# Placing work around a recurrent chain by a queue model that keeps an engine's occupation and a result's latency apart, with later low parts, SA copied by ScalarE and scores as a part of their own

## The chip, the cores and the metric

The kernel runs on one core of a Trainium2 chip. The metric is the device time of one execution in microseconds. The engines are called as the profile calls them: PE is TensorE (PEld its weight loads), DVE is VectorE, ACT is ScalarE, POOL is GpSimd, and SP is SyncE, which here only issues DMAs.

## The reference

One layer of a hybrid decoder runs on 2048 new tokens of a prompt and on 8 sequences of 4 tokens that have a state. The width is 1024, with 16 heads of 64.

```python
h = _rmsnorm(x, norm_g)
p = jnp.einsum('bsd,dn->bsn', h, w_in)
p_conv, p_rwkv, p_gate = _split(p, [N_CONV_COLS, N_RWKV_COLS, 2 * D_MODEL])
...
def step(S, inp):
    r_t, k_t, v_t, d_t, kk_t, a_t = inp
    sa = jnp.einsum('bhvk,bhk->bhv', S, -kk_t)
    S = (S * d_t[:, :, None, :] + sa[..., None] * (kk_t * a_t)[:, :, None, :]
         + v_t[..., None] * k_t[:, :, None, :])
    y = jnp.einsum('bhvk,bhk->bhv', S, r_t)
    return S, y
...
pc = jnp.einsum('bsc,cd->bsd', y_c, w_out_c)
pr = jnp.einsum('bsc,cd->bsd', y_r, w_out_r)
m = jax.nn.sigmoid(gc) * pc + jax.nn.sigmoid(gr) * pr
out = jnp.einsum('bsd,de->bse', m, w_o)
return x + out, ...
```

Beside the recurrent branch there is a short convolution branch (`y_c`). All is float32.

## The kernel before, in words

**Main stream.** The projections `p` are matmuls of weight blocks of 128 columns with the normalised input. To keep float32 accuracy with fast matmuls, each weight block and the input are split in a high and a low part, and three products are summed: `proj` issues, for each of eight k steps, high x high, low x high and high x low, 24 matmuls into one PSUM tile `ip`. The high part of a weight is a copy by ScalarE (`A.copy(hl[:, 0], raw)`), the low part a subtraction on VectorE (`w_lows`, tile `whl`). Both are stored, so that only the first of the four token sets (512 tokens each, the last with the 32 sample tokens added, called sets 0 to 3) splits weights; the others load the parts. `w_lows` is called at k step 2 of each block, and before a block's first use.

**Side jobs.** For each set and each of eight head pairs p there is a job per stage: *keys* (decay, scan, and the scaled keys AR, BK), *solve* (the scores `pt<-AR,BK`, their masking to GM, the 32 x 32 blocks Mc, their transpose Mi, and 31 pairs of operations tt, X that invert a triangular block), *merge* (the inverse Xbd), *load* (SV and BKt transposed) and *chain*. The chain carries the state S of a pair through 8 chunks of 64 tokens, one step each, and each link needs the one before: pa = AR x S on PE, us on DVE (two operations, one per head), pb = Xbd x us on PE, two copies into SV (`inner`: one by DVE, one by ACT), pb = BKt x SV on PE, S on DVE (two operations), and again pa. The matmuls of the main stream are put between the links, to cover them.

**Who decides the order.** The order of the instructions on each engine is that in which the Python code emits them, and a planner within the code decides it. `Traced` records each operation and its cost in `Clock`, which holds a time for each engine and for each part of a tile when it is ready. `drive` goes through the main stream matmul by matmul and, after each, lets each live `Side` run some steps: it runs when its goal (its share of the pair's stretch, from CUTS and SIDES) asks for it, when its next step's inputs are ready by the clock no later than PE's time (`due`), and, if it isn't one of the urgent kinds, when DVE is less than BACKLOG (1800) ahead of PE. `need` runs a job to its end when a tile must be free. Costs are by number of elements: for DVE 150 + 1.05 per element, for ACT 200 + 0.84. In `Clock.add` an engine is busy until the result is there, and what another engine reads is ready 60 later (200 behind PE). The framework's own scheduler moves rows of DVE and ACT a little afterwards.

All recorded operations have the line of the one call in `Traced`, L117 in the profile, so that the tiles tell them apart. `Queue` issues the DMAs on SP (L168).

After the last chain there is phase 3: the output projections `pc`, `pr` and `out`, again in split parts, with their 24 weights (tiles RH, RL, gt, ML, po) split on the way.

Of the kernel before, what the change touches and what calls it, by code (L numbers as in the profile page):

```python
# [23 lines left out]
HN = NT // 2  # L24
SIDES = {"first": 8.0, "late": 14.0, "keys": 30.0, "solve": 30.0, "merge": 8.0, "load": 8.0, "samp": 20.0, "out": 12.0, "prep": 10.0, "y": 4.0, "chain": 45.0, "zero": 1.0}

# [11 lines left out]
class Clock:  # L38
# [47 lines left out]

    def add(self, eng, outs, ins, cost, lag=60.0):
        start = max([self.t[eng]] + [e[4] for ap in ins for e in self._hits(ap) if e[6] != eng] +
                    [e[5] for ap in outs for e in self._hits(ap)])
        if eng == "POOL" or eng == "DVE" and sum(ap.space != PSUM for ap in ins) > 1:  # L90
            for s, e in self.held["POOL" if eng == "DVE" else "DVE"]:
                if s < start + cost and start < e:
                    start = e
            self.held[eng] = self.held[eng][-60:] + [(start, start + cost)]
        end = start + cost
        self.t[eng] = end
        for ap in ins:
            for e in self._hits(ap):
                e[5] = max(e[5], end)
        for ap in outs:  # L100
            for p0, p1, f0, f1 in self.boxes(ap):
                old = self.log.setdefault(self.name(ap), [])
                old[:] = [e for e in old if not (p0 <= e[0] and e[1] <= p1 and f0 <= e[2] and e[3] <= f1)][-95:]
                old.append([p0, p1, f0, f1, end + lag, end, eng])


class Traced:
# [18 lines left out]
    def cost(self, op, out, ins, k):  # L126
# [13 lines left out]
        if self.name == "DVE":  # L140
            per = {"transpose": 1.6, "tensor_tensor_scan": 2.1}.get(op, 1.05)
            if op == "tensor_reduce":
                n = ins[0].free_size()
            return 150 + per * n
        if self.name == "ACT":
            return 200 + 0.84 * n + 90 * max(0, len(ins) - 1)
        if k.get("op") == ALU.pow:
# [28 lines left out]
def hybrid_kernel(tc, x_prompt, x_sample, state_conv, state_shift, state_rwkv, norm_g, w_in, conv_w,  # L176
# [10 lines left out]
    NB = D // P  # L187
# [56 lines left out]

    def w_lows():
        while lows:
            hl, raw, keep = lows.pop(0)
            V.tensor_tensor(out=hl[:, 1], in0=raw, in1=hl[:, 0].bitcast(F32), op=ALU.subtract)
            SP.store(keep, hl.bitcast(F32))
# [12 lines left out]
    def proj(w, mov, c0, n):  # L262
# [3 lines left out]
        for kt in range(NB):  # L266
            if kt == 2:
                w_lows()
            for i, (w_, m_) in enumerate(((wh, mh), (wl, mh), (wh, ml))):
                T.matmul(ps[:, :n], lhsT=w_[:, kt, :], rhs=m_[:, kt], start=kt + i == 0, stop=kt == NB - 1 and i == 2)  # L270
                yield n / NT / 3
# [33 lines left out]
    class Side:  # L305
# [14 lines left out]

        def run(self, upto, force=False):
# [3 lines left out]
            while self.given < goal and self.f0 <= upto and (force or max(self.due, pt_free(self.banks)) <= clock.t["PE"] and (  # L325
                    self.kind in URGENT or clock.t["DVE"] < clock.t["PE"] + BACKLOG)):
                try:
                    x = next(self.g)
# [442 lines left out]
    def rkvz_blocks(th, p):  # L771
# [8 lines left out]
        def al(nm, bufs, kind, back):  # L780
            def alloc():
                need(job.get((kind, th * NB + p - back)))
                return rw.tile([P, NT + NSAMP], F32, name=nm, bufs=bufs)
# [20 lines left out]
    def rwkv_keys(th, p, o):  # L804
# [88 lines left out]
        for cvw, pw, ln, dst in parts:  # L893
# [11 lines left out]
        V.scalar_tensor_tensor(out=kh[:, 0:nt], in0=rT[:, 0:nt], scalar=rkh[:, p:p + 1], in1=kh[:, 0:nt],  # L905
                               op0=ALU.mult, op1=ALU.mult)
        yield W["key"], [kh[:, 0:nt]]
        bh = tmp.tile([P, TW], F32R, name="tmp")
# [16 lines left out]

    def rwkv_solve(th, p, o):

# [6 lines left out]
        for c0 in range(0, NCH + samp, 4):  # L934
# [12 lines left out]
            yield W["score"], (), 2 if c0 + 4 < NCH + samp else 0  # L947


# [23 lines left out]
        V.transpose(Xo.rearrange("p a e c -> p (a e c)"), X.rearrange("p a b -> p (a b)"))  # L973
        o.update(GM=GM, Xo=Xo, Mo=Mo)
        yield W["inv"]
# [385 lines left out]
    def begin_pair(th, p, total):  # L1361
# [174 lines left out]
```

## Time and profile before

| | |
|---|---|
| Median of 3 runs | 3245.81 us (3242.76 to 3250.17) |
| Profiled execution, its own time | 3239.32 us |
| Its span | 3237.6 us |
| Mean granted clock of PE | 0.987 |
| Instructions in the span | 54951 |
| Chain that ended last, by engine | PE 67%, DVE 20%, ACT 5%, issue 5%, DMA 2%, POOL 1% |
| DMA | 606.66 MB, mean 187 GB/s |

The page lists busy time per engine. In a row of the timeline stand the start, the duration, engine, line, operation, output tile <- input tiles, shape and how many are merged into the row, and in brackets how long the engine had been idle and who ended that. Rows of the waits name the waiting operation, what it waited for, the total in us, how often, and the longest. In the rows of the groups, after the bar, stand the busy time in us, the mean in ns, and the idle time of the engine ahead of the group, with what ended most of it. By the timeline, the first set runs to about 700 us, sets 1 and 2 from there to about 1900, set 3 to about 2608, the end of the last chain to about 2683, and phase 3 to the end.

### The profile page before, as it was taken

The page shows a single profiled execution, that of the slowest core. Times are in us where ns is not written, and L with a number is a line of the kernel's source. Part 1 is how long each engine was busy: PE and PEld are TensorE (multiplying, and loading weights), DVE is VectorE, ACT ScalarE, POOL GpSimd, SP SyncE. Part 2 cuts the span into 40 slices and gives each one's busy share as a digit, 9 for nine tenths or more (in the row PEclk, how much of TensorE's full clock was granted, in tenths as well). Part 3 has the DMA queues.
Part 4 walks back from the last instruction along what each step waited for, and adds up shares of the span by engine and source line. Part 5 has one row for each costly group of instructions (what it writes and reads, how often), then busy time and mean ns, then how long its engine had stood idle before and what let it go on. Part 6 is the DMA issues. An engine that isn't in the chain of part 4 may idle for free.

```text
span 3237.6 us, 54951 instructions
## 1 busy us (share of the span) xinstructions
PE 3109.5 (96%) x21234; PEld 2585.9 (80%) x21234; DVE 1999.7 (62%) x5703; ACT 1243.0 (38%) x2580; POOL 308.7 (10%) x517
## 2 busy tenths in 40 slices
PE   7999999999999999999999999999999969999998
PEld 6777777877777778777777899888898847788897
DVE  5687777776666657666666676666777745433332
ACT  5454544444334443443433344443444422211201
POOL 2011111110000111110001010100100000000000
PEclk9999999999999999999999999999999979999999
DMA  7786667644444444444444444434433339988773
GB/s 265 256 269 210 223 221 222 213 158 143 152 161 157 157 155 173 155 159 149 158 157 157 145 159 140 133 135 136 139 130 132 122 126 320 351 307 312 265 257 119
DMA packets 233308, 606.66 MB, mean 187 GB/s; under 512 B 32906, under 2 KB 136451, under 8 KB 179286
## 3 DMA queue, kind: packets, MB, share of 16 engines
q1 hardware_dynamic: 232902, 602.61, 54.4%
q8 instruction: 168, 2.75, 0.3%
q14 instruction: 94, 0.77, 0.1%
q0 software_dynamic: 144, 0.52, 0.0%
HBM read 447.90 MB, written 155.17 MB: 186 GB/s over the span
## 4 chain that ended last, share of the span: by engine, by line
PE 67%; DVE 20%; ACT 5%; issue 5%; DMA 2%; POOL 1%; SPq 0%; ACTq 0%; DVEq 0%; POOLq 0%
PE ip L117 48%; PE pt L117 10%; PE po L117 6%; DVE X L117 3%; DVE tt L117 3%; PE pb L117 3%; DVE tmp L117 2%; ACT tmp L117 2%; DVE Mi L117 2%; DVE whl L117 1%; DVE us L117 1%; DVE S L117 1%; PE pa L117 1%; ACT Xbd L117 1%; DVE GM L117 1%
## 5 line engine op out<-in xcount | busy, mean ns | idle before, releaser
L117 PE MATMUL ip<-XH,whl 128*128 128x512 f32 (+3 forms) x7408 | 2053.4, 356 | 6.6 <-DVE whl L117 1.9
L117 PEld LDWEIGHTS ip<-XH,whl 128*128 128x128 f32 x7408 | 1287.3, 190 | 183.2 <-issue 28.4
L117 PE MATMUL ip<-XL,whl 128*128 128x512 f32 (+3 forms) x3704 | 1316.1, 355 | 2.6 <-POOL XL L117 2.6
L117 PEld LDWEIGHTS ip<-XL,whl 128*128 128x128 f32 x3704 | 702.6, 190 | 80.4 <-issue 6.2
L117 DVE TENSOR_TENSOR X<-X,tt 128x60 f32<-128x60 f32 (+24 forms) x992 | 211.4, 213 | 27.4
L117 DVE TENSOR_TENSOR tt<-Mi,X 128x60 f32<-128x60 f32 (+24 forms) x992 | 209.8, 212 | 28.0
L117 DVE SCALAR_TENSOR_TENSOR S<-pb,pe,sp 64x64 f32<-64x64 f32 x512 | 143.6, 281 | 101.7 <-PE pb L117 95.5
L117 ACT ACTIVATE sp<-S,pe 128x128 f32<-128x128 f32 x256 | 99.5, 399 | 258.2 <-DVE S L117 254.9
L117 ACT ACTIVATE tmp<-ip,vec 128x512 f32<-128x512 f32 (+2 forms) x174 | 103.1, 593 | 231.4 <-PE ip L117 230.0
L117 ACT COPY SV<-pb 64x64 f32<-64x64 f32 x256 | 53.3, 208 | 330.2 <-DVE SV L117 326.3
L117 PE MATMUL ip<-RH,whl 128*128 128x512 f32 (+2 forms) x640 | 170.3, 355 | 4.9 <-ACT RH L117 4.9
L117 PE MATMUL po<-whl,MH 128*128 128x512 f32 x544 | 170.7, 394 | 1.2 <-ACT whl L117 1.1
L117 DVE TENSOR_TENSOR whl<-wraw,whl 128x1024 fp32r<-128x1024 f32 x105 | 134.2, 1279 | 53.3 <-ACT whl L117 52.8
L117 DVE SCALAR_TENSOR_TENSOR gt<-gt,ip 128x512 f32<-128x512 f32 (+1 forms) x80 | 46.9, 586 | 169.3 <-PE ip L117 167.1
L117 DVE TENSOR_TENSOR us<-pa,P 64x64 f32<-64x64 f32 x512 | 110.1, 215 | 57.5 <-PE pa L117 38.4
L117 ACT CAST whl<-wraw 128x1024 fp32r<-128x1024 f32 x105 | 109.5, 1044 | 60.6 <-DMA wraw<-in_w_out_r_dram 25.5
L117 PEld LDWEIGHTS pb<-us,Xbd 128*128 128x128 f32 x512 | 86.4, 190 | 57.6 <-PE ip L117 19.7
L117 PEld LDWEIGHTS ip<-RH,whl 128*128 128x128 f32 x640 | 112.8, 189 | 23.7 <-issue 4.0
L117 PEld LDWEIGHTS pb<-SV,BKt 128*128 128x128 f32 x512 | 85.3, 190 | 57.4 <-ACT SV L117 48.7
L117 PE MATMUL pb<-SV,BKt 128*128 128x128 f32 x512 | 108.1, 293 | 18.6 <-ACT SV L117 18.2
L117 PEld LDWEIGHTS po<-whl,MH 128*128 128x128 f32 x544 | 102.1, 188 | 25.6 <-ACT whl L117 1.6
L117 DVE TENSOR_TENSOR GM<-pt,mask_p 128x512 f32<-128x512 f32 x128 | 82.4, 685 | 61.4 <-PE pt L117 61.4
(489 smaller groups left out, 3940.5 us busy)
## 6 DMA issues: line engine op xcount, KB each, us to landing
wraw<-in_w_in_dram SPq DMA_DIRECT2D x81, 512.0 KB
whl<-w_k SPq DMA_DIRECT2D x24, 1024.0 KB
whl<-w_r SPq DMA_DIRECT2D x24, 1024.0 KB
whl<-w_v SPq DMA_DIRECT2D x24, 1024.0 KB
whl<-w_z SPq DMA_DIRECT2D x24, 1024.0 KB
whl<-w_xin SPq DMA_DIRECT2D x24, 1024.0 KB
whl<-w_cg SPq DMA_DIRECT2D x24, 1024.0 KB
whl<-w_zc SPq DMA_DIRECT2D x24, 1024.0 KB
```

The costliest lines, as they stand in the source:

```text
L117: r = f(*a, **k)
```

## The change

Five edits, all in the planner or in where an operation is put; the same matmuls are issued.

1. A cost may be a pair: the time for which the engine is taken, and the time until the result is there. DVE is taken for 80 less than its cost, ACT for 100 less. What an engine reads of its own results is waited for (to the end plus 30; not PE). The costs of DVE's transpose and of ACT are set anew.
2. `w_lows(late)`: from k step 2 a low part is queued when its cast is ready by the clock, and at the latest at k step 5. Before, it was queued at k step 2 whatever the cast.
3. In `inner`, ACT makes both SV copies.
4. The scores are a job of their own (`rwkv_scores`, "score"), with a stretch of its own ahead of the solve; the next pair's keys wait for the score instead of the solve.
5. `need_rows` runs a pair's keys, when its rT or kT tile must be free, only to the step that has read them.

```diff
     def add(self, eng, outs, ins, cost, lag=60.0):
+        taken, cost = cost if isinstance(cost, tuple) else (cost, cost)
         start = max([self.t[eng]] + [e[4] for ap in ins for e in self._hits(ap) if e[6] != eng] +
+                    [e[7] + 30 for ap in ins for e in self._hits(ap) if e[6] == eng != "PE"] +
                     [e[5] for ap in outs for e in self._hits(ap)])
...
         end = start + cost
-        self.t[eng] = end
+        self.t[eng] = start + taken
...
-                e[5] = max(e[5], end)
+                e[5] = max(e[5], start + taken)
...
-                old.append([p0, p1, f0, f1, end + lag, end, eng])
+                old.append([p0, p1, f0, f1, end + lag, start + taken, eng, end])
...
         if self.name == "DVE":
-            per = {"transpose": 1.6, "tensor_tensor_scan": 2.1}.get(op, 1.05)
...
-            return 150 + per * n
+            t = 150 + {"transpose": 1.85 if n > 512 else 1.15, "tensor_tensor_scan": 2.1}.get(op, 1.05) * n
+            return t - 80, t
         if self.name == "ACT":
-            return 200 + 0.84 * n + 90 * max(0, len(ins) - 1)
+            t = 150 + 0.85 * n + 95 * max(0, len(ins) - 1) + 40 * (ins[0].space != PSUM)
+            return t - 100, t
...
-    def w_lows():
-        while lows:
+    def w_lows(late=True):
+        while lows and (late or clock.ready([lows[0][0][:, 0]]) <= clock.t["DVE"]):
...
         for kt in range(NB):
-            if kt == 2:
-                w_lows()
+            if kt >= 2:
+                w_lows(kt >= NB - 3)
...
+    def need_rows(k):
+        sd = job.get(("keys", k))
+        if sd and not sd.ended:
+            need(*sd.after)
+            sd.run(float("inf"), True, lambda: outs[k].get("read"))
...
-        V.tensor_copy(SV[0:64, c, 0:64], pb[0:64, 0:64])
+        A.copy(SV[0:64, c, 0:64], pb[0:64, 0:64])
         A.copy(SV[0:64, c, 64:128], pb[64:128, 0:64])
...
-        job["keys", k] = Side(rwkv_keys(th, p, o), "keys", [prior("load", k - 1), prior("solve", k - 1)] + read(k - 2)).over(0, f[3])
-        job["solve", k] = Side(rwkv_solve(th, p, o), "solve", [job["keys", k], prior("merge", k - 1)] + read(k - 2)).over(f[3], f[4])
+        job["keys", k] = Side(rwkv_keys(th, p, o), "keys", [prior("load", k - 1), prior("score", k - 1)] + read(k - 2)).over(0, f[3])
+        mid = f[3] + 0.1 * total
+        job["score", k] = Side(rwkv_scores(th, p, o), "score", [job["keys", k]] + read(k - 2)).over(f[3], mid)
+        job["solve", k] = Side(rwkv_solve(th, p, o), "solve", [job["score", k], prior("merge", k - 1)]).over(mid, f[4])
```

What it does to the order is seen at three places on DVE. The first is in a steady pair of set 2, at the start of a chain; `tmp<-rst,tmp` is the scan of the keys job, S_471 the state of the chain, `ss` the keys' norms. Before:

```order
L117 TENSOR_TENSOR us<-pa,P_14314 64x64 x2
L117 TENSOR_SCALAR ss<-pt 128x8
L117 RECIPROCAL ss<-ss 128x8
L117 COPY SV<-pb 64x64
L117 SCALAR_TENSOR_TENSOR S_471<-pb,pe,sp 64x64 x2
L117 SCALAR_TENSOR_TENSOR tmp<-rst,tmp 128x512
L117 TENSOR_TENSOR us<-pa,P_14314 64x64 x2
```

The same place after the change:

```order
L120 TENSOR_TENSOR us<-pa,P_14314 64x64 x2
L120 TENSOR_SCALAR ss<-pt 128x8
L120 RECIPROCAL ss<-ss 128x8
L120 SCALAR_TENSOR_TENSOR tmp<-rst,tmp 128x512
L120 SCALAR_TENSOR_TENSOR S_471<-pb,pe,sp 64x64 x2
L120 TENSOR_TENSOR us<-pa,P_14314 64x64 x2
```

SV has left DVE, and the scan stands ahead of S. On PE, the lora matmuls whose result the scan needs stand two main matmuls earlier, ahead of pb.

The second place is in the same pair, where the solve begins (Mi, then the pairs tt, X). Before:

```order
L117 STREAM_TRANSPOSE Mi<-Mc 128x1024
L117 COPY SV<-pb 64x64
L117 TENSOR_TENSOR tt<-Mi,X 128x31
L117 TENSOR_TENSOR X<-X,tt 128x31
L117 TENSOR_TENSOR tt<-Mi,X 128x30
L117 TENSOR_TENSOR X<-X,tt 128x30
L117 TENSOR_TENSOR tt<-Mi,X 128x29
L117 TENSOR_TENSOR X<-X,tt 128x29
L117 TENSOR_TENSOR tt<-Mi,X 128x28
L117 SCALAR_TENSOR_TENSOR S_471<-pb,pe,sp 64x64 x2
```

And after the change:

```order
L120 STREAM_TRANSPOSE Mi<-Mc 128x1024
L120 TENSOR_TENSOR tt<-Mi,X 128x31
L120 TENSOR_TENSOR X<-X,tt 128x31
L120 TENSOR_TENSOR tt<-Mi,X 128x30
L120 TENSOR_TENSOR X<-X,tt 128x30
L120 TENSOR_TENSOR tt<-Mi,X 128x29
L120 TENSOR_TENSOR X<-X,tt 128x29
L120 TENSOR_TENSOR tt<-Mi,X 128x28
L120 TENSOR_TENSOR X<-X,tt 128x28
L120 SCALAR_TENSOR_TENSOR S_471<-pb,pe,sp 64x64 x2
```

Eight operations instead of seven stand between Mi and S. Between S and the next us there are seven instead of six.

The third place is the same point in a pair of set 0. Before:

```order
L117 SCALAR_TENSOR_TENSOR S_474<-pb,pe,sp 64x64 x2
L117 STREAM_TRANSPOSE Mi<-Mc 128x1024
L117 TENSOR_TENSOR us<-pa,P_4029 64x64 x2
L117 TENSOR_TENSOR tt<-Mi,X 128x31
L117 TENSOR_TENSOR X<-X,tt 128x31
L117 COPY SV<-pb 64x64
```

After the change (`whl<-wraw,whl` is a low part):

```order
L120 TENSOR_TENSOR us<-pa,P_3949 64x64 x2
L120 STREAM_TRANSPOSE Mi<-Mc 128x1024
L120 TENSOR_TENSOR tt<-Mi,X 128x31
L120 TENSOR_TENSOR X<-X,tt 128x31
L120 TENSOR_TENSOR whl<-wraw,whl 128x1024
L120 SCALAR_TENSOR_TENSOR S_474<-pb,pe,sp 64x64 x2
```

Mi stood ahead of us and now stands behind it, with a low part between it and S.

On PE, between two steps of the chain in a steady pair there were mostly six main matmuls from pa to pb, six to eight from pb to pb, and seven to the next pa; there now are six, six and seven. In the tail (the last pair's chain, with the last 48 main matmuls), four steps had no main matmul beside them and now three have none.

More of the change, by code (lines that the diff above doesn't have):

```diff
@@ L24 @@
 HN = NT // 2
-SIDES = {"first": 8.0, "late": 14.0, "keys": 30.0, "solve": 30.0, "merge": 8.0, "load": 8.0, "samp": 20.0, "out": 12.0, "prep": 10.0, "y": 4.0, "chain": 45.0, "zero": 1.0}
+SIDES = {"first": 8.0, "late": 14.0, "keys": 30.0, "score": 8.0, "solve": 22.0, "merge": 8.0, "load": 8.0, "samp": 20.0, "out": 12.0, "prep": 10.0, "y": 4.0, "chain": 45.0, "zero": 1.0}
 W = {"sq": 1.0, "norm": 1.0, "lora": 2.0, "one": 1.0, "scan": 2.0, "exp": 2.0, "key": 1.0, "bones": 1.5,
@@ L91, in add @@
             for s, e in self.held["POOL" if eng == "DVE" else "DVE"]:
-                if s < start + cost and start < e:
+                if s < start + taken and start < e:
                     start = e
-            self.held[eng] = self.held[eng][-60:] + [(start, start + cost)]
+            self.held[eng] = self.held[eng][-60:] + [(start, start + taken)]
         end = start + cost
-        self.t[eng] = end
+        self.t[eng] = start + taken
         for ap in ins:
             for e in self._hits(ap):
-                e[5] = max(e[5], end)
+                e[5] = max(e[5], start + taken)
         for ap in outs:
@@ L319, in over, with run @@
             return self
-        def run(self, upto, force=False):
+        def run(self, upto, force=False, passed=None):
             if any(not x.ended for x in self.after) or upto < self.f0:
@@ L326, in run @@
                     self.kind in URGENT or clock.t["DVE"] < clock.t["PE"] + BACKLOG)):
+                if passed and passed():
+                    break
                 try:
@@ L781, in alloc @@
             def alloc():
-                need(job.get((kind, th * NB + p - back)))
+                if kind == "keys":
+                    need_rows(th * NB + p - back)
+                else:
+                    need(job.get((kind, th * NB + p - back)))
                 return rw.tile([P, NT + NSAMP], F32, name=nm, bufs=bufs)
@@ L906, in rwkv_keys @@
                                op0=ALU.mult, op1=ALU.mult)
+        o["read"] = True
         yield W["key"], [kh[:, 0:nt]]
@@ L924, in hybrid_kernel, with rwkv_scores @@
     blk = [(slice(64 * h + 32 * b, 64 * h + 32 * b + 32)) for h in range(2) for b in range(2)]
-    def rwkv_solve(th, p, o):
+    def rwkv_scores(th, p, o):
         AR = o["AR"]
@@ L947, in rwkv_solve @@
             yield W["score"], (), 2 if c0 + 4 < NCH + samp else 0
+        o["GM"] = GM
+    def rwkv_solve(th, p, o):
+        GM = o["GM"]
         Mc = rw.tile([P, NCH, 32], F32, name="Mc")
@@ L973, in rwkv_solve @@
         V.transpose(Xo.rearrange("p a e c -> p (a e c)"), X.rearrange("p a b -> p (a b)"))
-        o.update(GM=GM, Xo=Xo, Mo=Mo)
+        o.update(Xo=Xo, Mo=Mo)
         yield W["inv"]
```

## The prediction

> **What bounds the kernel now.** I read the page's busy times first, then the busy time by stretches, then TensorE's (PE's) waits, and last the timeline at two chain steps.
>
> ```profile
> PE 3109.5 (96%) x21234; PEld 2585.9 (80%) x21234; DVE 1999.7 (62%) x5703; ACT 1243.0 (38%) x2580; POOL 308.7 (10%) x517
> ```
>
> PE is busy 96% of the span, with the same matmuls before and after the change, so only its idle time can go. The stretches (busy us of PE, PEld, DVE, ACT, POOL, then granted clock, DMA share, GB/s) show where it lies: sets 1 and 2, the end of the last chain, and phase 3.
>
> ```profile
> 700.00:1900.00 1200.00, 1176.74 (x7891) 938.03 (x7892) 779.09 (x2355) 484.97 (x1021) 130.13 (x231) 1.00 0.45 156
> 2608.00:2683.00 75.00, 46.50 (x225) 30.03 (x224) 38.14 (x87) 22.27 (x51) 5.58 (x4) 0.68 0.39 128
> 2683.00:3237.00 554.00, 538.76 (x2667) 452.41 (x2667) 204.06 (x383) 96.67 (x177) 11.43 (x17) 0.99 0.77 277
> ```
>
> The waits of PE over the whole run (total, times, longest) name what the change can reach: the three links of the chain.
>
> ```profile
> PE pb L117 <- DVE us L117: 23.8, 41, 1.6
> PE pb L117 <- ACT SV L117: 18.2, 29, 1.4
> PE pa L117 <- DVE S L117: 4.8, 8, 0.9
> ```
>
> They sum to 46.8 us, 1.4% of the run, and that is the whole prize of a better order. Per pair they are small. The first two lines below are all of the chain's waits in a steady pair (1379.00 to 1453.80), the next two those in a pair of set 0 (462 to 540), where weights are still split.
>
> ```profile
> PE pb L117 <- ACT SV L117: 0.7, 1, 0.7
> PE pb L117 <- DVE us L117: 0.3, 1, 0.3
> ...
> PE pb L117 <- DVE us L117: 1.7, 2, 1.1
> PE pb L117 <- ACT SV L117: 0.4, 1, 0.4
> ```
>
> The rows understate a stall a little, since the modelled end of the matmul ahead of it reaches into it: about 0.16 us each (below, pb1 due at 1418.74 + 1.62 = 1420.36 starts at 1420.78, 0.42 late, and its row says 0.26).
>
> **Part by part.** *SA copied by ScalarE.* VectorE (DVE) loses 256 copies, ScalarE gains 256:
>
> ```profile
> L117 DVE COPY SV<-pb 64x64 f32<-64x64 f32 x256 | 53.3, 208 | 38.2 <-PE pb L117 36.2
> L117 ACT COPY SV<-pb 64x64 f32<-64x64 f32 x256 | 53.3, 208 | 330.2 <-DVE SV L117 326.3
> ```
>
> ScalarE's copy already waited for VectorE's (326.3 us of idle time, by the second row), so the two ran one after the other, 0.42 us in all; two on ScalarE take the same 0.42. What goes is the case in which VectorE comes late to its copy: 0.7 idle per steady pair, about 0.85 with the hidden part. It is 53 us off an engine that is not the bound, and 53 us onto one that is busy 38%.
>
> *The order around the chain, steady pairs.* Rows at two places of one steady pair; pa, us, pb, SV, pb, S, pa is one step:
>
> ```profile
> 1386.48 0.38 PE L117 MATMUL pb<-SV,BKt 128*128 128x128 f32 x2
> 1386.90 0.58 DVE L117 SCALAR_TENSOR_TENSOR S<-pb,pe,sp 64x64 f32<-64x64 f32 x2 [2.70 <-PE pb L117]
> 1387.03 0.63 ACT L117 ACTIVATE tmp<-tmp 128x512 f32<-128x512 f32 x1
> 1387.76 1.22 DVE L117 TENSOR_TENSOR_SCAN tmp<-rst,tmp 128x512 f32<-128x512 f32 x1 [0.28 <-ACT tmp L117]
> 1388.34 0.38 PE L117 MATMUL pa<-S,AR 128*128 128x128 f32 x2
> ...
> 1413.41 0.38 PE L117 MATMUL pa<-S,AR 128*128 128x128 f32 x2
> 1413.83 0.45 DVE L117 TENSOR_TENSOR us<-pa,P 64x64 f32<-64x64 f32 x2
> 1414.31 2.07 DVE L117 STREAM_TRANSPOSE Mi<-Mc 128x1024 f32<-128x1024 f32 x1
> 1415.03 0.33 PE L117 MATMUL pb<-us,Xbd 128*128 128x64 f32 x2
> 1416.42 0.19 DVE L117 TENSOR_TENSOR tt<-Mi,X 128x31 f32<-128x31 f32 x1
> ...
> 1416.78 0.49 PE L117 MATMUL pb<-SV,BKt 128*128 128x128 f32 x2
> 1417.77 0.19 DVE L117 TENSOR_TENSOR tt<-Mi,X 128x28 f32<-128x28 f32 x1
> 1417.87 0.57 DVE L117 SCALAR_TENSOR_TENSOR S<-pb,pe,sp 64x64 f32<-64x64 f32 x2
> 1418.74 0.38 PE L117 MATMUL pa<-S,AR 128*128 128x128 f32 x2
> ...
> 1419.94 0.21 DVE L117 TENSOR_TENSOR X<-X,tt 128x50 f32<-128x50 f32 x1
> 1420.19 0.45 DVE L117 TENSOR_TENSOR us<-pa,P 64x64 f32<-64x64 f32 x2
> 1420.78 0.41 PE L117 MATMUL pb<-us,Xbd 128*128 128x64 f32 x2 [0.26 <-DVE us L117]
> ```
>
> From them: pa starts 0.42 before us (1413.41, 1413.83); pa to pb1, with six main matmuls (ip) between, 1.62; pb2 to S 0.42 and, with seven matmuls, to the next pa 1.86 (1386.48, 1388.34), so an ip is 1.86 / 8 = 0.233. A solve operation takes 0.225 (six steps from 1416.42 to 1417.77), the wider ones about 0.24. us ends 0.14 before pb1 can start.
>
> Scan first: the order now puts the scan ahead of S, and the lora matmuls two ip (0.47) earlier. So the scan is ready near 1387.76 - 0.47 = 1387.29 and ends at 1388.51. S then ends 0.58 later, less 0.08 of overlap, at 1389.01, and pa comes at 1389.06 instead of 1388.34: +0.72.
>
> Solve: with SV gone, eight solve operations instead of seven stand between Mi and S, so S starts at 16.42 + 8 x 0.225 = 18.22 and ends at 18.80; pb2 is free to go at 15.03 + 1.62 = 16.65, its pa is due at 18.51, and comes at 18.85, 0.33 late. Seven operations instead of six stand ahead of the next us, which ends at 18.80 + 1.69 + 0.48 = 20.97 while pb1 is due at 18.85 + 1.62 = 20.47: with the 0.14, 0.64 late. The third step has 0.13 left. Sum 1.1.
>
> After: 1.1 + 0.72 = 1.8 a pair. Before: 0.85 for SV, 0.43 for us, 0.1 at 1418.74, 1.4. So +0.4 a pair, and +6 us over the 14 pairs of sets 1 and 2 that repeat this order.
>
> *Set 0.* Mi stood ahead of us there, and pb waited:
>
> ```profile
> 414.87 2.05 DVE L117 STREAM_TRANSPOSE Mi<-Mc 128x1024 f32<-128x1024 f32 x1 [0.61 <-ACT Mc L117]
> 416.95 0.45 DVE L117 TENSOR_TENSOR us<-pa,P 64x64 f32<-64x64 f32 x2
> 417.54 0.41 PE L117 MATMUL pb<-us,Xbd 128*128 128x64 f32 x2 [1.12 <-DVE us L117]
> ```
>
> That is about 1.3 with the hidden part. Now us goes first, and Mi, two solve operations and often a low part stand between us and S: 2.05 + 0.45 + 1.2 = 3.7 from us's end at pa + 0.87, so S is done at pa + 5.2 against pa due at 1.62 + 1.62 + 1.86 = 5.1. That costs 0.1 to 0.15; other places of the new order, where a low part lands ahead of S, give back about as much again. I take -1.0 a pair, for 7 pairs -7 us (bounds -1.3 and +0.4, the steady loss).
>
> *Low parts.* Each low part takes 1.28 us, and VectorE sat idle ahead of it for the cast, 52.8 us in 105:
>
> ```profile
> L117 DVE TENSOR_TENSOR whl<-wraw,whl 128x1024 fp32r<-128x1024 f32 x105 | 134.2, 1279 | 53.3 <-ACT whl L117 52.8 <-DMA xo<-in_x_prompt_dram 0.2
> PE ip L117 <- DVE whl L117: 1.9, 2, 1.1
> ```
>
> Queued when the cast is due, it blocks nothing behind it; that is part of set 0's gain above. Forced at the sixth of eight k steps, it has nine matmuls, 9 x 0.233 = 2.1 us, before its use (18 and 4.2 before the change). 2.1 covers 1.28 with 0.8 of queue, so +1 us (bounds 0 and +5: the second row's 1.9 more than doubled). In phase 3 VectorE is busy 37%, so nothing there.
>
> *Last set and tail.* Set 3 has its own order, with gains and losses as above: +1.5 (bounds -4 and +6). In the tail the chain's last steps have no matmuls left beside them:
>
> ```profile
> 2630.14 0.38 PE L117 MATMUL pa<-S,AR 128*128 128x128 f32 x2
> 2633.29 0.49 PE L117 MATMUL pa<-S,AR 128*128 128x128 f32 x2 [0.69 <-DVE S L117]
> ```
>
> A bare step is 3.15 us. The 48 matmuls left are spread thinner: bare steps fall from four to three, and 3 + 2 + 4 instead of 3 + 5 + 4 lie in the others. One bare step and a half us in three others: -4 (bounds -6 and 0). The score's own part and the rule for key rows change only where things are placed, which the order above already contains.
>
> **One rule against the change.** The new planner lets each VectorE operation free the engine 80 ns before its result. Full ones do overlap so; the chain's pair us, 0.45 against 2 x 0.215, does not:
>
> ```profile
> 1408.41 1.29 DVE L117 TENSOR_TENSOR GM<-pt,mask_p 128x512 f32<-128x512 f32 x2 [0.96 <-PE pt L117]
> L117 DVE TENSOR_TENSOR GM<-pt,mask_p 128x512 f32<-128x512 f32 x128 | 82.4, 685 | 61.4 <-PE pt L117 61.4
> L117 DVE TENSOR_TENSOR us<-pa,P 64x64 f32<-64x64 f32 x512 | 110.1, 215 | 57.5 <-PE pa L117 38.4 <-ACT P L117 10.1 <-ACT tmp L117 2.2
> ```
>
> The Trainium skill (VectorE: DVE Perf Modes, "Two Vector instructions with no wait between them") says that an operation whose start quadrant differs from that of the operation before it starts only when all earlier ones have finished. The two halves of us and S start in different quadrants, so the trace agrees. By that rule the planner books each pair 0.16 short, and the sum stands as worked out; by the planner's own 80 ns the three late operations of a steady pair would each come 0.16 sooner, and the sum would be 14 x 3 x 0.16 = 7 us lower.
>
> **Sum.** +6 - 7 + 1 + 1.5 - 4 = -2.5 us on the profiled 3239.3, or 3236.8. That execution lies 0.2% under the median of 3245.8, so the forecast on the median's scale is 3245.8 x 3236.8 / 3239.3 = 3243: no change, as about 0.2% (6.5 us) is what a measurement of this kernel can tell.
>
> **Rivals.** *Slower, scan and late S everywhere.* If the new order's places (scan ahead of S, eight and seven solve operations) cost their 0.4 in all 32 pairs and set 0 gains nothing: 13, +5 for low parts, 18 us, 3264. It decides where a chain operation ends later than the 1.62 and 1.86 of cover. For: steady cover falls to six matmuls everywhere, and the 0.16 per pair; against: set 0's Mi was the largest single wait.
>
> *Faster, the better model pays.* If half of the 46.8 us of chain waits goes, 3222. For: SV's 18.2 loses its cause, and 52.8 us of blocked VectorE time in the low parts; against: the two places above.
>
> *Low parts late.* If 30 of the 105 low parts, forced late, each hold ip up for 1 us: +30, about 3273. For: 0.8 us of slack only; against: the 1.9 row.
>
> *It does not do what it says.* The framework reorders rows after the planner, so what is modelled better isn't what runs; all of it drowns: 3246.
>
> **How the numbers follow.** Forecast 0.40 (its own range 3231 to 3255: faster 0.09, same 0.26, slower 0.05), slower rival 0.18, faster rival 0.27, low parts 0.08, nothing 0.07. Faster 0.36, same 0.33, slower 0.31. The range 3222 to 3264 reaches to both main rivals' times and leaves out the low parts' case and the outer half of the faster one.
>
> **What would show it.** Right: waits of pb for SV near nothing; pa for S up from 4.8 to 15 or more, with the scan or solve operations ahead of S; pb for us down in set 0, about 0.6 a steady pair; pa to end of the tail some 4 us shorter. Wrong: chain waits well under 30 us together with a shorter stretch 700 to 1900 (faster), or ip waiting for whl in tens of us (low parts).

## The result, and the profile after

The changed kernel takes 3281.8 us (median) against 3242.8 of the kernel before: a ratio of 1.0116, 95% interval 1.0097 to 1.0135. That is some 38 us slower, outside the range. One execution, the one first profiled, was disturbed and is left out of the ratio (12873 us, PE's matmuls at a quarter of their speed), so the profile read here is of a further run of the same code, the first of the experiments: span 3282.1 us, ratio 1.0104 (1.0087 to 1.0122). For before the profile is the one shown above, span 3237.6 us.

The page's busy times after the change:

```profile
PE 3139.4 (96%) x21234; PEld 2604.7 (79%) x21234; DVE 1945.3 (59%) x5439; ACT 1294.0 (39%) x2844; POOL 290.7 (9%) x517
```

The same 21234 matmuls keep PE busy 29.9 us longer (3109.5 before), and the span is 44.5 longer. So a third of the loss at most is idle time that a list of waits can show; the greater part is matmuls that run longer. The waits of PE over the run that bear on the argument, after the change:

```profile
PE pb L120 <- DVE us L120: 19.0, 47, 1.4
PE pa L120 <- DVE S L120: 15.5, 27, 1.5
...
PE pt L120 <- ACT BKt L120: 7.8, 4, 2.2
PE pb L120 <- ACT SV L120: 6.8, 16, 0.8
PE pt L120 <- DVE T L120: 6.7, 8, 1.5
PE pt L120 <- DVE tmp L120: 5.5, 11, 1.6
PE ip L120 <- ACT whl L120: 5.4, 2, 4.9
```

The chain's three waits fell from 46.8 to 41.3 us: S rose from 4.8 to 15.5, as forecast, and SV's fell from 18.2 to 6.8, where near nothing was forecast. What grew is what stands in the side jobs and the weights: `pt` for ACT's BKt (7.8, none before), for T (3.0 before), for DVE's tmp (3.5 before), and `ip` for ACT's whl (1.3 before).

To see where time is lost, take the start of the same main matmul (the n-th of the 11112 `ip` matmuls of sets 0 to 3 and what follows with XH, XL) in both traces. By the kernel's own list of blocks, set 0 ends at 0.205 of them, set 2 at 0.581 and set 3 at 0.914. At 0.267 the two orders have done the same side work too, as many side matmuls each. In us behind before:

```
main matmuls done    0.267                 0.600           0.933              1.000
which is             3 pairs into set 1    behind set 2    behind the tail    the last
changed kernel       2.2                   11.1            44.8               44.5
```

2 us are lost in set 0 and the first three pairs of set 1, 9 in the rest of sets 1 and 2, 34 in the last set and the tail, none in phase 3. The last set, by stretches of busy time (us of PE, PEld, DVE, ACT, POOL, granted clock, DMA share, GB/s), before and after:

```profile
1946.00:2608.00 662.00, 642.79 (x5760) 592.16 (x5759) 451.73 (x1493) 268.64 (x650) 58.58 (x85) 1.00 0.40 135
```

```profile
1957.00:2658.00 701.00, 669.61 (x5805) 612.84 (x5805) 440.86 (x1430) 283.76 (x722) 56.22 (x87) 0.97 0.38 129
```

PE is busy 27 us more and idle 12 more, and its granted clock, 1.00 before, is 0.97. The waits of PE in the last set after the change:

```profile
PE pt L120 <- ACT BKt L120: 7.8, 4, 2.2
PE pt L120 <- ACT tmp L120: 4.3, 8, 1.6
PE pb L120 <- DVE us L120: 2.9, 8, 0.7
PE pt L120 <- ACT SV L120: 2.8, 5, 0.7
```

Before, no wait for BKt or SV by `pt` stood there. How one of 2.2 us comes about, from the timeline after the change:

```profile
2351.80 2.75 ACT L120 COPY Xbd<-Xo 32x256 f32<-32x256 f32 x4 [2.55 <-DVE Xo L120]
...
2354.56 0.40 ACT L120 COPY X<-X 128x256 f32<-128x256 f32 x1
2354.98 0.25 ACT L120 COPY SV<-pt 32x128 f32<-32x128 f32 x1
2355.24 0.27 ACT L120 COPY BKt<-pt 128x128 f32<-128x128 f32 x1
...
2355.56 0.30 PE L120 MATMUL pt<-ident,Yc 128*64 128x128 f32 x1 [2.19 <-ACT BKt L120]
```

Four copies on 32 partitions take 2.75 us of ScalarE, 0.69 each, one after the other. The planner books each with 0.41 until its result and 0.31 of occupation, 1.23 for the four, so by its clock BKt's copy, which frees the PSUM bank that `pt` needs, is done 1.5 us sooner than it is. So it places the matmul too early, and PE stands behind it.

What can follow a stall is seen a little earlier, around a wait of 1.1 us of `pt` for ACT's Wm that ends at 2186.78. PE's waits from 2180 to 2205, and then stretches of 4 us, the third number from the right the granted clock:

```profile
PE pt L120 <- ACT Wm L120: 1.1, 1, 1.1
PE pt L120 <- ACT tmp L120: 0.4, 1, 0.4
...
2184.00:2188.00 4.00, 2.74 (x54) 2.31 (x47) 1.83 (x5) 2.34 (x7) 1.11 (x3) 1.00 0.52 162
2188.00:2192.00 4.00, 4.00 (x23) 3.39 (x23) 1.09 (x6) 0.88 (x3) 0.00 (x0) 0.72 0.43 174
2192.00:2196.00 4.00, 3.59 (x10) 1.76 (x8) 0.29 (x1) 1.27 (x2) 0.00 (x0) 0.50 0.00 0
2196.00:2200.00 4.00, 4.00 (x45) 3.55 (x45) 1.70 (x3) 1.41 (x4) 0.00 (x0) 0.50 0.34 68
2200.00:2204.00 4.00, 4.00 (x22) 4.00 (x22) 1.95 (x5) 2.93 (x9) 0.33 (x2) 0.58 0.69 281
2204.00:2208.00 4.00, 4.00 (x31) 3.58 (x30) 3.50 (x10) 1.61 (x6) 0.00 (x0) 1.00 0.02 4
```

The clock drops to a half some 3 us after the stall and stays there for 13.7 us (2189.7 to 2203.4 in stretches of 0.5), in which 6.8 us are lost by PE, six times the stall. Adding up stretch width times (1 - clock) gives 18.8 us lost in this way in the last set after the change and 1.7 before. I call this the time lost to the clock.

### The profile page after: what moved, and what is told of

The parts are those of the page before. It is cut to its first block, busy times and chain, and to the rows that moved or that the text cites. A ratio compares the mean times of both kernels' runs of the same rounds, so it can differ in the third digit from the quotient of the medians.

```text
span 12871.6 us, 55001 instructions
## 1 busy us (share of the span) xinstructions
PE 12819.3 (100%) x21234; PEld 9164.9 (71%) x21234; DVE 1974.9 (15%) x5439; ACT 1296.7 (10%) x2844; POOL 277.2 (2%) x517
## 3 DMA queue, kind: packets, MB, share of 16 engines
q8 instruction: 168, 2.75, 0.1%
## 4 chain that ended last, share of the span: by engine, by line
PE 100%; DVE 0%; POOL 0%; ACT 0%; issue 0%; ACTq 0%; DVEq 0%; POOLq 0%
PE ip L120 77%; PE pt L120 12%; PE po L120 5%; PE pb L120 3%; PE pa L120 2%; DVE xo L120 0%; ACT tmp L120 0%; DVE tmp L120 0%; DVE nw L120 0%; POOL tmp L120 0%; DVE Yc L120 0%; DVE sq L120 0%; DVE mu__28999 L120 0%; POOL mu__28999 L120 0%; DVE S L120 0%
## 5 line engine op out<-in xcount | busy, mean ns | idle before, releaser
L120 PE MATMUL ip<-XH,whl 128*128 128x512 f32 (+3 forms) x7408 | 7501.3, 1146 | 0.7 <-DVE whl L120 0.7
L120 PEld LDWEIGHTS ip<-XH,whl 128*128 128x128 f32 x7408 | 4488.9, 638 | 1434.8 <-issue 1361.3
L120 PE MATMUL ip<-XL,whl 128*128 128x512 f32 (+3 forms) x3704 | 4220.7, 1140 | 0.0
L120 PEld LDWEIGHTS ip<-XL,whl 128*128 128x128 f32 x3704 | 2359.2, 637 | 693.0 <-issue 661.2
L120 PE MATMUL po<-whl,MH 128*128 128x512 f32 x544 | 523.5, 1099 | 0.0
L120 PE MATMUL ip<-RH,whl 128*128 128x512 f32 (+2 forms) x640 | 515.3, 943 | 3.4 <-ACT RH L120 3.4
L120 PEld LDWEIGHTS pa<-S,AR 128*128 128x128 f32 x512 | 335.5, 672 | 141.9 <-issue 136.8
L120 PE MATMUL pa<-S,AR 128*128 128x128 f32 x512 | 346.0, 831 | 1.4 <-DVE S L120 1.4
L120 PE MATMUL pt<-AR,BK 64*128 64x128 f32 x1056 | 306.8, 797 | 0.0
L120 PE MATMUL ip<-RL,whl 128*128 128x512 f32 (+2 forms) x320 | 297.8, 932 | 0.0
```

What stands on the lines that cost most here:

```text
L120: r = f(*a, **k)
```

## The experiments

In the table are the median, the ratio to before with its interval, and from the profiled execution of each the us behind before at the same main matmul. Runs e13 to e16 put a single edit into the kernel before; the others start from the changed kernel. The last four columns come from one execution each: e4 and e11, which are the same up to the last set, stand 2.6 to 2.8 us apart there, so a difference of 3 us in a column shows nothing by itself.

```
run                   us      ratio (interval)         0.267  0.600  0.933  1.000
e1_after              3279.2  1.0104 (1.0087-1.0122)     2.2   11.1   44.8   44.5
e2_sv_dve             3286.7  1.0133 (1.0118-1.0148)    14.4   20.7   45.9   45.1
e3_lows_old           3290.2  1.0145 (1.0130-1.0161)    14.3   23.7   52.6   54.8
e4_clock_old          3234.4  0.9969 (0.9959-0.9979)    -1.0   -3.2   -6.5   -5.2
e5_no_overlap         3249.7  1.0019 (1.0009-1.0028)     5.2   14.6   14.0   14.9
e6_narrow             3266.9  1.0073 (1.0058-1.0088)     3.9   15.2   25.7   26.8
e7_old_last           3248.7  1.0012 (1.0002-1.0022)     2.0   10.3   10.7   11.3
e8_new_mid            3238.6  0.9986 (0.9976-0.9995)    -8.3   -0.3    0.2    1.2
e9_narrow_xbd         3262.2  1.0057 (1.0042-1.0072)     3.0   16.0   19.1   18.9
e10_xbd_only          3276.6  1.0097 (1.0076-1.0119)     0.4    9.7   37.5   38.2
e11_late_act          3241.9  0.9992 (0.9980-1.0005)     1.8   -0.6    2.6    4.4
e12_old_xbd           3228.0  0.9951 (0.9937-0.9966)    -3.0   -3.7  -10.4  -10.0
e13_sv_only           3243.3  1.0005 (0.9995-1.0015)     3.8   -1.0    1.9    2.2
e14_lows_only         3256.2  1.0050 (1.0035-1.0065)    15.6   18.0   19.8   19.5
e15_costs_only        3273.1  1.0104 (1.0089-1.0119)    11.2   17.6   33.6   33.9
e16_score_rows_only   3269.8  1.0092 (1.0076-1.0107)    14.0   18.5   28.6   29.0
```

**e1_after.** No edit.

> The changed kernel unchanged, for a profile. It is some 36 to 40 us slower than before (1.012). Theory A (late chain operations): the waits of PE for us, SV and S grow from 46.8 us to 80 or more, spread over the pairs of sets 1 and 2. Theory B (low parts late): ip waits for whl grow from 2 us to tens, all before 620 us. Theory C (clock): the waits stay about the same, and PE's matmuls are longer at a lower granted clock in some stretch.

Measured above. The chain's waits did not double (A as worded falls), the whl waits are 5.4 us and not tens (B falls), and the clock is lower in the last set (C holds for half of the loss there).

**e2_sv_dve.** One edit undone:

```diff
-        A.copy(SV[0:64, c, 0:64], pb[0:64, 0:64])
+        V.tensor_copy(SV[0:64, c, 0:64], pb[0:64, 0:64])
```

> SV's first copy back on VectorE, all else as changed. If ScalarE's two copies in a row are the loss (a copy behind a cast or behind Mc there), this takes back most of the 38 us: 3250 or less. By theory A it takes back nothing, since the planner's short costs stay: 3275 to 3290, with some waits for SV back. By theory B also nothing.

It takes nothing back (7 us more); the two copies on ScalarE are not the loss.

**e3_lows_old.** The low parts' rule undone:

```diff
-            if kt >= 2:
-                w_lows(kt >= NB - 3)
+            if kt == 2:
+                w_lows()
```

> Low parts queued at k step 2 again, all else as changed. Theory B: back to about 3245. Theory A: no change in sets 1 to 3, where no low part is, and at most some us in set 0: 3270 to 3285.

It loses 11 us more, most of it ahead of 0.267; low parts forced late are not the loss.

**e4_clock_old.** The queue model undone, the four other edits kept:

```diff
-                    [e[7] + 30 for ap in ins for e in self._hits(ap) if e[6] == eng != "PE"] +
...
-            return t - 80, t
+            return 150 + {"transpose": 1.6, "tensor_tensor_scan": 2.1}.get(op, 1.05) * n
...
-            return t - 100, t
+            return 200 + 0.84 * n + 90 * max(0, len(ins) - 1)
```

> The planner's costs, its one time for occupation and result, and its free reads of an engine's own results as before; SV, low parts, score part and key rows as changed. Theory A: back to 3235 to 3250, the whole loss being the new model. Theories B and C (if the cause is another edit): stays near 3280.

3234.4 us, 0.3% faster than before. So beside the other edits the model is the whole loss, some 45 us, and together they gain 10 without it.

**e5_no_overlap and e6_narrow** split the model: an engine is taken until its result is there, for all operations, or only for those on fewer than 128 partitions.

```diff
-            return t - 80, t
+            return t
...
-            return t - 100, t
+            return t
```

```diff
-            return t - 80, t
+            return (t if out.ap[0][1] < P else t - 80), t
...
-            return t - 100, t
+            return (t if out.ap[0][1] < P else t - 100), t
```

> The engine is taken until its result is there (no 80 or 100 less), the new costs and the waits for own results kept. If the short occupation is the cause, VectorE's and ScalarE's queues are modelled as long as they are and the loss in the last set goes: about 3240. Rival: the occupation is not the cause, but the new costs and the waits for own results: stays at 3270 or more.

> The 80 and 100 less only for operations on all 128 partitions, since those on 32 or 64 did not overlap in the trace. If it is these operations that the changed planner books too short, most of the loss goes, as with no overlap at all: about 3240. Rival, that full operations matter as much: halfway, about 3260; rival, that occupation does not matter: 3270 or more.

Without any overlap 28 to 31 us are back by the ratios, and the last set loses nothing (14.6 at 0.600, 14.0 at 0.933). What is left against e4_clock_old, some 15 us and by the traces most of it ahead of 0.600 (17.8 us behind e4 there, 20.5 at 0.933), belongs to the new costs and the waits for own results, which no run parts from each other. With overlap on full operations only, 10 to 14 us are back. So short occupation is the cause in the last set, and narrow operations are not all of it. In e6_narrow the wait for BKt in the last set was still there, nearly whole:

```profile
PE pt L120 <- ACT BKt L120: 6.9, 4, 2.1
```

**e7_old_last and e8_new_mid** use the old costs in the last set alone, and the new ones in sets 1 and 2 alone, by a switch where the jobs of a pair are made (with the old costs it also turns the waits for own results off):

```diff
+        clock.old = th == LAST
```

```diff
+        clock.old = th in (0, LAST)
```

> The old planner costs in the last set alone, the new ones in sets 0 to 2. The traces show the changed kernel 40 us behind in the last set and some 10 us behind up to there. If the sets add, 3240. If the loss there comes from the state that the earlier sets leave behind, it stays near 3280.

> The new planner costs in sets 1 and 2 alone, the old ones in set 0 and in the last. Against the kernel with old costs throughout (3234), the changed kernel is 7 us faster over sets 1 and 2. If the sets add, 3227; if the place of a set's work is chance and not the model's doing, anything from 3227 to 3245.

e7_old_last gives back 30 us, all of it in the last set (10.3 at 0.600, 10.7 at 0.933). e8_new_mid is 8.3 us ahead at 0.267 and loses 8 from there to 0.600, as the changed kernel loses 9 there. Before the run I had read from the traces that the new costs gain 7 in these sets; that reading had put the border between sets 0 and 1 where the two orders stand at different side work. But what the new costs cost in sets 1 and 2 is read against e4_clock_old, which has the same set 0 (both are 9.6 ahead of before at 0.205, with the same side work done). From there to 0.267 e4 loses 8.6 us and e8 1.2, with 6.8 and 3.4 of it lost to the clock; from 0.267 to 0.600 e4 gains 2.2. At 0.600 e8 is 2.9 us behind e4, about what two executions of the same code differ by. So against the old costs the new ones lose 10 us from 0.267 to 0.600, and over both sets as a whole 3 us or nothing.

**e9_narrow_xbd and e10_xbd_only** book the copy Xbd<-Xo with what it takes, the first in e6_narrow, the second in the changed kernel:

```diff
-            t = 150 + 0.85 * n + 95 * max(0, len(ins) - 1) + 40 * (ins[0].space != PSUM)
+            t = 150 + 0.85 * n + 95 * max(0, len(ins) - 1) + 40 * (ins[0].space != PSUM) + 280 * (len(out.ap) > 3)
```

> As the run with overlap on 128 partitions only, and ScalarE's copy Xbd<-Xo (four of them, 32 partitions) booked at the 0.69 us that the traces show instead of 0.41. In that run the last set still had three waits of PE for BKt of about 2 us, right behind these copies. If their price is the rest of the loss: those waits go, the last set is at most 10 us behind before, and the time is 3240 to 3250. If not: 3260 or more.

> The changed kernel, with only the copy Xbd<-Xo booked 0.28 us longer; the 80 and 100 less stay for all. If this one copy is most of the loss in the last set: 3250 or less. If the many short bookings add up: between, 3258 to 3272. If it is not it: 3275 or more.

Alone the true price of this copy gives back 3 us at most, which the intervals don't part from nothing. With the narrow operations it brings the last set and the tail to a loss of 3 us (16.0 to 19.1), against 34 in the changed kernel, though 16 stay from the sets before, so the total missed what was expected (the execution in the trace is the fastest of four, 4 us under their median). The stretch of the last set and the wait in it:

```profile
1962.00:2635.00 673.00, 654.15 (x5805) 599.05 (x5803) 444.83 (x1430) 284.56 (x722) 55.75 (x86) 1.00 0.40 134
```

```profile
PE pt L120 <- ACT BKt L120: 2.3, 2, 2.0
```

This stretch has the same 5805 PE instructions as the changed kernel's. It is 28 us shorter: 15.5 less busy, at a clock of 1.00 instead of 0.97, and 12.5 less idle. In time lost to the clock it is 1.7 us against 18.8. A third part stays in e9: the score matmuls take longer, for a reason that e14_lows_only shows below. From 0.600 to 0.914, in us more than before, "scores" being the time from the start of each score or bones matmul to that of PE's next one, idle time left out:

```
                       all    clock   idle   scores
e1_after              33.9     17.1   10.3      5.6
e10_xbd_only          29.9     15.4    7.2      5.2
e6_narrow             12.8      3.4    3.1      4.8
e9_narrow_xbd          6.1      0.0   -2.2      4.6
e5_no_overlap         -1.9     -1.7   -3.4     -0.2
e7_old_last           -2.1     -1.7   -5.4      1.1
e16_score_rows_only    7.3      1.7    2.2      2.3
```

So of the loss in the last set half is the clock, some 10 us are the stalls themselves, and 6 are scores. The parts nearly add up to the whole. More idle time mostly goes with more time lost to the clock, but e16 shows that an order made with the old costs can lose 7 us here too: how much of a single run's loss is its own edit, and how much its order, these runs tell only for differences well above that.

**e11_late_act** adds work to ScalarE's queue that the planner does not book, in e4_clock_old. The added copies repeat work and change no value:

```diff
+            if samp and i > 1:
+                nc.scalar.copy(Xbd[g, 0:NCH, g].rearrange("p c (a e) -> p c a e", e=4),
+                               Xo[g].rearrange("p a e c -> p c a e"))
```

> The kernel with the old planner costs (3234), with two of the four copies Xbd<-Xo made twice in the last set's eight pairs, not booked in the planner: 1.37 us more of ScalarE's queue per pair than the planner knows, as much as the changed planner books these four copies short (4 x 0.34). This adds work of no use. If a queue that is longer than booked makes PE wait there, and the waits lower the granted clock: waits up by 8 to 16 us, a clock below 1.00 in the last set, and in all 15 to 40 us slower. If PE's stalls cost only their own time: the rise equals the rise of the waits, 8 to 16. If there is slack: 0 to 3.

3241.9 against 3234.4, 7.5 us slower. In the trace the last set and the tail lose 6.5 (from -0.6 to 2.6, and from -3.2 to -6.5 without): 3 us more of idle time and 3.4 more lost to the clock. The kind of damage looks like that of the changed kernel, stalls and as much again by the clock, but its size is a fifth, and 3.4 us to the clock are lost in this set by e13 and e16 too, without these copies. So one queue that runs 1.4 us late per pair does not do it alone.

**e12_old_xbd** is e4_clock_old with the true price of that copy:

```diff
-            return 200 + 0.84 * n + 90 * max(0, len(ins) - 1)
+            return 200 + 0.84 * n + 90 * max(0, len(ins) - 1) + 280 * (len(out.ap) > 3)
```

> The old planner costs with only Xbd<-Xo booked 0.28 us longer, the other edits as changed. If a truer price helps where it was too short: 3225 to 3232. If the old costs' surplus on other operations already covers it: 3234 as without. If a new order of the last set is mostly chance: anything from 3228 to 3245.

3228.0 us, 0.5% faster than before, and the lowest median of all. Against e4_clock_old it is 6 us, with intervals that overlap a little (0.9937 to 0.9966, 0.9959 to 0.9979).

**e13_sv_only to e16_score_rows_only** put one edit each into the kernel before: SV's copy (as in the diff of e2_sv_dve, the other way round), the low parts' rule, the costs, occupation and own waits, and the score part with the key rows' rule.

> The kernel before, with only SV's first copy moved to ScalarE. Before had 18.2 us of waits for SV. If they go and nothing comes in their place: 10 to 18 us faster than before, 3226 to 3235. If the planner's new order turns them into other waits: within 5 us of before.

> The kernel before, with only the low parts' rule. If the gain of set 0 comes from it: 3232 to 3238, all of it ahead of 670 us. If a low part forced late makes ip wait: slower by 2 to 8.

> The kernel before, with only the planner's new costs, occupation and own waits. If the model is bad for this kernel whatever the other edits: 3265 to 3290, with the loss in the last set and a lower clock there. If it is bad only beside ScalarE's 256 further copies, which it books short as well: 3240 to 3255.

> The kernel before, with only the scores as a part of their own and the key rows' rule. If these let the keys start earlier and spread VectorE's work: 3232 to 3240. If not: within 5 us of before.

The costs alone lose 32 us, so the model is bad here with or without ScalarE's 256 further copies. 16 of them are lost in the last set and the tail, with the same wait:

```profile
PE pt L120 <- ACT BKt L120: 6.6, 4, 1.8
```

But no other edit gains alone: SV's copy is even, the low parts' rule loses 15 us, the score part and key rows 28. Together, with the old costs, they gain 10. So the edits do not add, and a loss of 45 us by the model holds only beside the others. Where one of these losses comes from can be read. In e14_lows_only 15.1 us are lost by the end of set 0, where score matmuls look like this, first in the kernel before, then in e14_lows_only:

```profile
251.45 1.16 PE L117 MATMUL pt<-AR,BK 64*128 64x128 f32 x16
...
254.13 1.16 PE L117 MATMUL pt<-AR,BK 64*128 64x128 f32 x16
```

```profile
260.12 0.71 PE L117 MATMUL pt<-AR,BK 64*128 64x128 f32 x4
...
260.76 0.51 PE L117 MATMUL pt<-tmp,bones 128*128 128x512 f32 x1
261.20 0.71 PE L117 MATMUL pt<-AR,BK 64*128 64x128 f32 x4
...
263.65 1.71 PE L117 MATMUL pt<-AR,BK 64*128 64x128 f32 x16
...
265.59 1.16 PE L117 MATMUL pt<-AR,BK 64*128 64x128 f32 x8 [0.23 <-DVE GM L117]
```

The two heads' matmuls use half of the array's rows each (64 of 128). In the kernel before half of them start 0.01 us after the one ahead, as the code issues the heads in turn, so that 16 take 1.16. In e14 they come in fours between the bones matmuls, mostly 0.11 apart, and 16 take 1.71: one head's, then the other's, as I read it (the rows do not name the head, and that the bones matmul holds one head's PSUM bank up is not shown). With idle time left out, score matmuls take 31.5 us of set 0 instead of 18.1, and bones matmuls 6.6 instead of 3.8: together 16 more, as much as the 15 lost. PE's idle time by the trace is the same (40.0 and 40.9), which is why no list of waits shows it. In e16_score_rows_only the same parts are spread over the run: up to 0.933 it is 12 us more idle, loses 7 more to the clock and 10 more by scores, of 28.6 in all.

## Why the prediction was wrong, point by point

**The bound.** That only PE's idle time can go was wrong. PE's busy time holds two things that an order changes: the granted clock (18.8 us lost in the last set, 1.7 before) and whether matmuls on half of the rows run in pairs (16 us in set 0 of e14_lows_only). So the 46.8 us of chain waits bound neither the prize nor the penalty. Neither of the two signs of being wrong that the prediction named came (the chain's waits are 41.3 us, `ip`'s for whl no tens): both look at waits alone.

**Steady pairs: right.** The order came out nearly to the tenth of a microsecond as worked. The rows after the change, at the two places:

```profile
1393.08 0.38 PE L120 MATMUL pb<-SV,BKt 128*128 128x128 f32 x2
...
1393.90 1.23 DVE L120 TENSOR_TENSOR_SCAN tmp<-rst,tmp 128x512 f32<-128x512 f32 x1 [4.12 <-ACT tmp L120]
1395.04 0.56 DVE L120 SCALAR_TENSOR_TENSOR S<-pb,pe,sp 64x64 f32<-64x64 f32 x2
...
1395.65 0.49 PE L120 MATMUL pa<-S,AR 128*128 128x128 f32 x2 [0.55 <-DVE S L120]
...
1425.14 0.49 PE L120 MATMUL pa<-S,AR 128*128 128x128 f32 x2
1426.85 0.45 DVE L120 TENSOR_TENSOR us<-pa,P 64x64 f32<-64x64 f32 x2
1427.44 0.41 PE L120 MATMUL pb<-us,Xbd 128*128 128x64 f32 x2 [0.41 <-DVE us L120]
```

S stands behind the scan, and pa comes at 1395.65 where 1393.08 + 1.86 = 1394.94 was due: 0.71 late, forecast 0.72. pb comes at 1427.44 where 1425.14 + 1.62 = 1426.76 was due: 0.68 late, forecast 0.64. From 0.267 to 0.600, some 14 pairs, 8.9 us were lost (2.2 to 11.1), forecast 6; PE's idle time rose by 5.1 there. The list of waits shows less: the chain's three went from 19.3 to 20.8 us in sets 1 and 2, SV's 13.0 gone and us and S up from 6.3 to 20.8.

**Set 0: the wait went, the gain did not come.** Waits of pb for us fell from 10.8 to 2.4 us there, as worked out. But in their place PE waits once 4.9 us for a cast, which ScalarE starts late, and for T 4.7, SV 3.8 and S 3.5 (before 1.7, 2.6 and none). Ahead of that cast ScalarE stood idle for 5.2 us, until VectorE's tmp was there at 129.47, and then made the four Xbd copies (2.66 us):

```profile
133.22 1.04 ACT L120 CAST whl<-wraw 128x1024 fp32r<-128x1024 f32 x1
...
134.31 0.80 PE L120 MATMUL ip<-XH,whl 128*128 128x512 f32 x1 [4.92 <-ACT whl L120]
```

Forecast -7, measured +2 by 0.267. The step that failed is "other places of the new order, where a low part lands ahead of S, give back about as much again": it looked at DVE and the chain only, not at ScalarE and the merge job. With the old costs in set 0 (e4_clock_old and e8_new_mid) this set ends 9.6 us ahead of before. But only 4 to 5 us of that are idle time; the clock takes 1.7 and 5.1 us in place of 11.9, which no edit aimed at. So of the forecast's 7 us from waits at most 5 came out, and none in the changed kernel.

**Low parts: right in size beside the other edits.** whl's late parts cost no tens of us (e3_lows_old), and `ip`'s wait for VectorE's whl went from 1.9 to 1.4 us. Alone in the kernel before, the rule costs 15 us (e14_lows_only), by the order of the score matmuls, which the term did not have.

**The last set: the term that failed.** "Set 3 has its own order, with gains and losses as above: +1.5 (bounds -4 and +6)" measured +34 with the tail. I had worked no place of it by hand. The mechanism was in the text, as the rule against the change, but only for DVE's chain pairs and with 0.16 us each. In the last set it is ScalarE's merge copies and the many operations on 32 and 64 partitions, booked 0.1 to 0.4 us short each, with main matmuls of about half the length to cover them (256 to 296 columns instead of 512). e5_no_overlap and e7_old_last show the cause (short occupation, in the last set). With true prices for the narrow operations and that copy, 31 of the 34 us are gone (e9_narrow_xbd). What the term put at nothing without a reason is PE's busy time: of the 34 us, 17 are lost to the clock and 6 in the scores, and 10 are idle time.

**The tail: right in sign.** The last chain's eight steps took 29.8 us (2654.47 to 2684.28) instead of 31.84: -2.0, forecast -4.

```profile
2654.47 0.49 PE L120 MATMUL pa<-S,AR 128*128 128x128 f32 x2
...
2684.28 0.47 PE L120 MATMUL pt<-ident,S 128*128 128x128 f32 x1 [0.69 <-DVE S L120]
```

**The rivals.** The time of the low parts' rival, 3273, counts from the forecast of 3243, those of the other two from the median of 3246. The slower one had the right sign and the wrong place: scan ahead of S cost its price, but the loss beyond it was ScalarE's queue in the last set, with the clock and the scores. The faster one, that a better model pays, is refuted for this model (e4_clock_old, e15_costs_only); whether a truer price pays where it makes an operation longer is not settled (e12_old_xbd, 6 us with intervals that overlap).

**What stays open.** Why PE's clock drops after one cluster of stalls and not after another of the same length: before had one of 1.11 us at 2408.35 without a drop, and of the changed kernel's three waits for BKt of 2.2 us (2355.56, 2444.76, 2532.79) the last had none. That stalls start the drops is argued from their place in time and from the table under e9, not shown. And why the three other edits lose alone and gain together is shown for the low parts alone (score matmuls out of pairs); for the score part the loss is split above, but what in the order makes it was not followed. What the transpose's and ACT's new costs do apart from the waits for own results was not run either.

## What to carry to other kernels

In this kernel costs that were too short put waits on the critical engine (some 30 us by e5_no_overlap), while the old, longer ones did not: when occupation and latency are split, check both against the trace for each class of operation, by partitions and access pattern, before any is shortened. Where matmuls fill 96% of a span, a sum by idle rows alone can miss most of a loss: look at the granted clock and at the spacing of small matmuls too. An edit to such a planner moves every later decision, so each stage needs its own look, the densest first.

## What the runs showed of the hardware

- After a stall of 1.1 us the granted clock was 0.50 for 13.7 us. The time lost to the clock from 0.600 to 0.914 was 1.7 us before, 3.4 in e11, 5.1 in e6, 8.5 in e2, 13.7 in e3, 17.1 in e10 and 18.8 in e1: steps of 1.7 us, a half of 3.4 us. The Trainium skill (TensorE: Matmul & The Clock Gate, "HAM oscillation — how this bites in real kernels") gives idle gaps of more than about 3.4 us as the rule for such a drop. The step of 3.4 us agrees; that no single gap was longer than 1.1 us there differs, and the measurement decides.
- ScalarE's four copies Xbd<-Xo on 32 partitions, which write a strided output and read Xo in another order than it lies, took 2.75 us in a row, 0.69 each for 256 elements, where the copies Mc<-GM of the same size took 0.40. Which of the two patterns costs the time was not parted.
- Matmuls on half of the rows each start 0.01 us apart in pairs where the code's turn of the two heads is kept (16 in 1.16 us), and mostly 0.11 apart where it is not (16 in 1.71).
